# Norm weights spread by a product with ones, and a waiting expert's raw weights asked for behind unit 1's rows

## The chip, the cores and the metric

The kernel runs on one core of one Trainium2 chip. The core has five engines that run side by side and wait for each other through semaphores: TensorE (PE, matmul), VectorE (DVE), ScalarE (ACT), GpSimd (POOL) and SyncE (SP, which issues DMAs); sixteen DMA engines move the data. The metric is device time in microseconds of one execution. Times of runs are given as medians; durations of single instructions come from one profiled execution.

## What is computed

One layer of a hybrid trunk on x of 512 rows and 1024 columns, fp32 in and out. It is a norm, a combined projection into three mixers, an output product, then a mixture of experts, then a last norm:

```python
h = rms_norm(x, norm1_g[l])
proj = h @ w_in[l]
y_ssm  = ssm_mixer(proj[..., :s0], ...)        # 256 columns, diagonal state space, GLU
y_pool = pool_mixer(proj[..., s0:s1], ...)     # 256 columns, causal means over 2, 4, 8, 16
y_att  = moba_attention(q, k, v, rel_bias)     # 8 heads of 64, blocks of 256, relative bias
x = x + concatenate([y_ssm, y_pool, y_att]) @ w_out[l]
h = rms_norm(x, norm2_g[l])
x = x + hier_moe(h, ...)                       # 4 groups of 4 experts, best group, best 2 in it
return rms_norm(x, final_norm_g)

def rms_norm(x, g):
    y = xf * lax.rsqrt(jnp.mean(xf * xf, axis=-1, keepdims=True) + RMS_EPS)
    return y * g
```

Each expert is `silu(h @ w_gate) * (h @ w_up) * weight @ w_down` with 256 inner columns.

## The kernel before

Rows are worked on in four blocks of 128 (`NT`). Products with large weights are made in fp16: each fp32 weight half tile (128 x 1024, 512 KB) is loaded into one of five staging slots (`STG`) and split into a high and a low fp16 part, and a product runs in three passes (high·high, high·low, low·high). The high part is made by ScalarE; the low part by VectorE in one SCALAR_TENSOR_TENSOR or, where `less_busy(1.0)` finds VectorE over 1 us more loaded than GpSimd in the planner's model, by GpSimd, for which ScalarE makes one more pass that scales the slot in place.

The order of all work is set when the program is built. `Flow` (L71 on) is a planner: every stage is a coroutine that yields the engine it wants, the events it needs and the tokens (buffers) it takes; the planner keeps a modelled time for each engine and for DMA, and lets the coroutine go that can start first, by rank where several can. Changing one stage's needs or cost can so move any other instruction on any engine, and can change which splits go to GpSimd.

Start: `s_first_loads` (L419) issues on SP the four x blocks and the small constants; `s_norm1` (L495) takes the squares (ScalarE), the scale (GpSimd) and the product with the scale and the norm weights `g1` (VectorE, tile `xp`), then 8 transpositions (`pt`) and the split into `hT`. The weights of the projection follow as v, u, q, k, p, q, k, v (tiles `w_v`, `w_u`, `w_q`, `w_k`, `w_p`, products `ps_v`, `pu`, `ps_q`, `ps_k`, `ps_p`). Meanwhile VectorE prepares the SSM's powers (`sm`, `pw`, `bb`, `bl`) and the attention's bias: a one-hot product `pb` of two parts is copied from PSUM into `scr`, SP stores it (`t_scr`) and reads it back in eight broadcast DMAs (`tb`). `psS` are attention scores, `pr` probabilities, `ptp` their transpositions.

Experts: after the second norm and the routing, GpSimd scatters the rows into `x_scr` by expert (96 slots for each of 16 experts). They are worked on in units of 128 slots: unit 0 holds expert 0 and 32 slots of expert 1, unit 1 64 of expert 1 and 64 of expert 2, and so on. Unit 0 is gathered on chip by products (`gb`); later units read their rows from `x_scr` (`s_xt`, L1605, tile `xr`, for unit 1 in `xp_123`), transpose them (`tx`, then `xts`), make gate and up products (`pg`), Silu (`xs`), its transposition (`pta`, `aT`), the down product (`py`), and scatter `ys` to `y_scr`. The weights of experts come through the five slots in order (`s_exp_loads`), each with gate, up and down in two half tiles. Gate and up of experts 5 and 6 (`RAW`) are loaded without a split into spare pages (`s_raw_loads`, L1548, tile `raw`) while the attention's weights give their space free; they are split later into pages that earlier units have done with: expert 5 into that of expert 0, 6 into raw 5's, expert 7 into raw 6's. `s_xt` needs the scatters to have landed. All loads but GpSimd's scatters are issued by SP, in the order in which they stand.

## Time and profile before

| what | value |
|---|---|
| time, median of 3 runs | 431.93 us (429.52 to 432.06) |
| the profiled execution | 431.17 us, its span 429.4 us |
| TensorE busy | 364.4 us (85%) |
| VectorE busy | 321.7 us (75%) |
| ScalarE busy | 236.1 us (55%) |
| GpSimd busy | 54.6 us (13%) |
| moved by DMA | 110.33 MB, 257 GB/s in the mean |
| granted TensorE clock, mean | 0.949 |

The span is what the profiler records between first and last instruction; 1.8 us of the profiled execution lie around it. In a timeline each row is a start, a duration, an engine, a line (nearly all L96, a helper that records every operation), the operation with its output and inputs, and in brackets how long the engine sat idle before it and what released it. A row with x2 or more groups neighbours. SPq is SP's queue of issues: its durations are those of issuing, not of the transfer.

### The profile page before, as it was taken

The page shows a single profiled execution, that of the slowest core. Times are in us where ns is not written, and L with a number is a line of the kernel's source. Part 1 is how long each engine was busy: PE and PEld are TensorE (multiplying, and loading weights), DVE is VectorE, ACT ScalarE, POOL GpSimd, SP SyncE. Part 2 cuts the span into 40 slices and gives each one's busy share as a digit, 9 for nine tenths or more (in the row PEclk, how much of TensorE's full clock was granted, in tenths as well). Part 3 has the DMA queues.
Part 4 walks back from the last instruction along what each step waited for, and adds up shares of the span by engine and source line. Part 5 has one row for each costly group of instructions (what it writes and reads, how often), then busy time and mean ns, then how long its engine had stood idle before and what let it go on. Part 6 is the DMA issues. An engine that isn't in the chain of part 4 may idle for free.

```text
span 429.4 us, 8450 instructions
## 1 busy us (share of the span) xinstructions
PE 364.4 (85%) x3272; PEld 204.9 (48%) x3272; DVE 321.7 (75%) x649; ACT 236.1 (55%) x400; POOL 54.6 (13%) x87
## 2 busy tenths in 40 slices
PE   2799897399998999999799878699999875678991
PEld 1598453164454466554376754345445431333340
DVE  2798866967854778777578887989788887777382
ACT  4754132346757796937463216867677756565131
POOL 1200000420500000000034520122111010000020
PEclk9999999599999999999899988899999998689997
DMA  8935599950798998558855899838999997989924
GB/s 278 354 115 151 167 146 187 380 168 4 157 181 262 300 355 312 182 156 268 302 197 204 299 418 351 288 118 291 404 331 359 406 337 256 321 279 350 396 97 152
DMA packets 49384, 110.33 MB, mean 257 GB/s; under 512 B 4507, under 2 KB 25755, under 8 KB 49340
## 3 DMA queue, kind: packets, MB, share of 16 engines
q1 hardware_dynamic: 46188, 100.07, 72.1%
q0 software_dynamic: 2592, 9.44, 5.4%
q10 hardware_dynamic: 560, 0.25, 0.5%
q8 instruction: 27, 0.44, 0.4%
q14 instruction: 17, 0.14, 0.1%
HBM read 85.04 MB, written 24.69 MB: 256 GB/s over the span
## 4 chain that ended last, share of the span: by engine, by line
PE 50%; DMA 24%; DVE 13%; ACT 5%; issue 4%; SPq 1%; POOL 0%; POOLq 0%; ACTq 0%; DVEq 0%
PE px L96 7%; DMA st_lde<-in_moe_w_down_dram 7%; PE pg L96 6%; PE py L96 5%; DMA st_lde<-in_moe_w_gate_dram 4%; PE pf L96 4%; PE ps_v L96 4%; DVE gu L96 4%; DMA st_lde<-in_moe_w_up_dram 4%; DMA xs<-in_glu_w_dram 3%; PE psS L96 3%; PE pu L96 3%; PE ptp L96 3%; PE ps_k L96 3%; DVE dn L96 2%
## 5 line engine op out<-in xcount | busy, mean ns | idle before, releaser
L96 DVE SCALAR_TENSOR_TENSOR gu<-st_lde,gu 128x1024 f16<-128x1024 f32 x55 | 68.0, 1251 | 15.9 <-ACT gu L96 15.6
L96 PE MATMUL pg<-gu,xts 128*32 128x512 f16 (+1 forms) x960 | 71.7, 395 | 8.6 <-ACT gu L96 7.2
L96 ACT ACTIVATE gu<-st_lde 128x1024 f16<-128x1024 f32 x56 | 58.2, 1056 | 16.4 <-DMA st_lde<-in_moe_w_up_dram 11.1
L96 PEld LDWEIGHTS <-xts 128*32 128x32 f16 (+1 forms) x960 | 31.1, 103 | 44.0 <-issue 20.4
L96 PE MATMUL px<-wo,cat 128*128 128x512 f16 x192 | 45.6, 389 | 2.4 <-ACT wo L96 1.8
L96 PE MATMUL py<-dn,aT 128*32 128x512 f16 (+1 forms) x480 | 39.0, 420 | 8.8 <-ACT aT L96 7.5
L96 DVE SCALAR_TENSOR_TENSOR dn<-st_lde,dn 128x1024 f16<-128x1024 f32 x32 | 38.6, 1218 | 2.4 <-ACT dn L96 1.8
L96 ACT ACTIVATE dn<-st_lde 128x1024 f16<-128x1024 f32 x32 | 33.2, 1053 | 7.6 <-DMA st_lde<-in_moe_w_down_dram 7.5
L96 PEld LDWEIGHTS <-hT 128*64 128x64 f16 (+1 forms) x384 | 30.7, 155 | 5.1 <-issue 1.4
L96 PEld LDWEIGHTS <-cat 128*128 128x128 f16 x192 | 18.9, 100 | 24.3 <-issue 6.0
L96 PEld LDWEIGHTS <-aT 128*32 128x32 f16 (+1 forms) x480 | 14.8, 105 | 30.1 <-ACT aT L96 9.7
L96 ACT ACTIVATE pr<-pr,nm 128x128 f32<-128x128 f32 (+3 forms) x32 | 17.9, 562 | 15.0 <-DVE nm L96 14.8
L96 POOL DMA_INDIRECT y_scr<-ys,tok x10 | 11.9, 1190 | 103.9 <-ACT ys L96 78.6
L96 PE MATMUL ps_v<-w_v,hT 128*128 128x256 f16 x192 | 24.1, 282 | 1.0 <-ACT hT L96 0.6
L96 PE MATMUL ps_q<-hT,w_q 128*128 128x512 f16 x96 | 22.6, 380 | 0.0
L96 PE MATMUL ps_k<-hT,w_k 128*128 128x512 f16 x96 | 22.2, 380 | 0.0
L96 PE MATMUL ptp<-cpk,pr 128*128 128x128 f32 x80 | 13.6, 284 | 9.5 <-DVE pr L96 9.3
L96 DVE CUSTOM_DVE_ANT_0 pr<-psS,tb 128x128 f32<-128x128 f32 (+3 forms) x32 | 15.5, 485 | 7.7 <-DMA xs<-in_glu_w_dram 3.8
L96 ACT COPY pts<-ptp 128x128 f32<-128x128 f32 (+3 forms) x32 | 12.7, 424 | 12.5 <-PE ptp L96 12.4
L96 PEld LDWEIGHTS ptp<-cpk,pr 128*128 128x128 f32 x80 | 9.2, 141 | 17.4 <-DVE pr L96 9.4
L96 ACT ACTIVATE xs<-xp 128x512 f32<-128x512 f32 (+1 forms) x12 | 9.2, 770 | 14.5 <-DVE xp L96 10.7
L96 DVE TENSOR_TENSOR xts<-tx,xts 128x512 f16<-128x512 f32 x22 | 14.7, 685 | 2.4 <-ACT xts L96 2.1
(242 smaller groups left out, 633.3 us busy)
## 6 DMA issues: line engine op xcount, KB each, us to landing
st_lde<-in_moe_w_down_dram SPq DMA_DIRECT2D x32, 512.0 KB
st_lde<-in_moe_w_gate_dram SPq DMA_DIRECT2D x28, 512.0 KB
st_lde<-in_moe_w_up_dram SPq DMA_DIRECT2D x28, 512.0 KB
x_scr<-zero SPq DMA_DIRECT2D x12, 512.0 KB
xr<-x_scr SPq DMA_DIRECT2D x10, 512.0 KB
xp<-in_x_dram SPq DMA_DIRECT2D x8, 512.0 KB
y_scr<-zero SPq DMA_DIRECT2D x8, 512.0 KB
yr<-y_scr SPq DMA_DIRECT2D x4, 1024.0 KB
```

The lines of the kernel that those rows point to most:

```text
L96: r = f(*args, **kw)
```

## The change

The norm weights are no longer broadcast by a DMA of 128 x 1024. One row of 1 x 1024 is loaded first on SP, ahead of x; two fp32 products of a row of ones with its halves write it to all partitions in PSUM, and VectorE copies them into `g1`. The raw loads of expert 6 wait also for the event that unit 1's rows have been asked for.

```diff
     def s_first_loads():
+        yield "sp"
+        sp.dma_start(g1[0:1, :], a["norm1_g"])
+        fl.sig_dma("g1r")
         for t in range(NT):
...
             if t == 0:
-                yield "sp"
-                sp.dma_start(g1, a["norm1_g"].to_broadcast([P, D]))
-                fl.sig_dma("g1")
                 yield "sp"
                 sp.dma_start(cpk, a["cpk"])
...
+    def s_g1():
+        one = scr_a[0:1, 0:P]
+        yield "dve"
+        v.memset(one, 1.0)
+        for nh in range(2):
+            half = slice(nh * 512, (nh + 1) * 512)
+            yield "pe", ("g1r",), ("mm",)
+            pg = bank("mm", f"pg1_{nh}")
+            pe.matmul(pg, one, g1[0:1, half], start=True, stop=True)
+            yield "dve"
+            v.tensor_copy(g1[:, half], pg)
+            fl.give("mm")
+        fl.sig("g1")
...
-                    yield "sp", (("wo_end", 1),), ("fly",)
+                    yield "sp", (("wo_end", 1),) if e == RAW[0] else (("wo_end", 1), "xr_rows"), ("fly",)
...
             fl.sig_dma(("xr", u))
+            if u == NG:
+                fl.sig("xr_rows")
...
     fl.spawn(2, s_first_loads())
+    fl.spawn(0, s_g1())
```

The planner then orders the program anew. Seven splits go to GpSimd where one did: both halves of `w_q` and the first of `w_k` of the first pair of heads, one gate half of expert 2, one down half of expert 5, and two halves (gate and up) of expert 7, which had one there already.

VectorE, start, before: the first rows that read x or weights (`xp` is an x block times its scale and `g`, first block 0; `w_v` the low half of the first weights; `hT` the low half of x's transposition).

```order
L96 SCALAR_TENSOR_TENSOR xp_122<-xp_122,rs_174,g_126 128x1024
L96 SCALAR_TENSOR_TENSOR w_v_179<-st_ld_v_0_157,w_v_179 128x1024
L96 SCALAR_TENSOR_TENSOR hT_111<-pt_0_182,hT_110 128x4x128
L96 SCALAR_TENSOR_TENSOR hT_111<-pt_1_189,hT_110 128x4x128
L96 SCALAR_TENSOR_TENSOR w_v_179<-st_ld_v_1_159,w_v_179 128x1024
L96 SCALAR_TENSOR_TENSOR xp_122<-xp_122,rs_199,g_126 128x1024
```

And now:

```order
L96 MEMSET scr_112 1x128
L96 COPY g_126<-pg_0_169 128x512
L96 COPY g_126<-pg_1_175 128x512
L96 SCALAR_TENSOR_TENSOR w_v_183<-st_ld_v_0_158,w_v_183 128x1024
L96 SCALAR_TENSOR_TENSOR xp_122<-xp_122,rs_181,g_126 128x1024
L96 SCALAR_TENSOR_TENSOR w_v_183<-st_ld_v_1_160,w_v_183 128x1024
```

The first split of w_v has moved ahead of x block 0.

VectorE, the end of the bias preparation, before (`w_k` is a split, `ptu` a transposition of u, `pb` the two bias products; the store of the table waits for the second copy of `pb`):

```order
L96 COPY bbd<-bb 64x16x16 x2
L96 SCALAR_TENSOR_TENSOR w_k_648<-st_ld_k_0_416,w_k_648 128x1024
L96 TENSOR_TENSOR scr_112<-bb,pw 128x1024
L96 COPY xp_123<-ptu_651 128x512
L96 TENSOR_TENSOR bl_682<-bb,pw 128x1024
L96 SCALAR_TENSOR_TENSOR w_k_648<-st_ld_k_1_419,w_k_648 128x1024
L96 COPY xp_123<-ptu_684 128x512
L96 TENSOR_TENSOR bl_682<-bl_682,scr_112 128x1024
L96 COPY scr_113<-pb_645 128x512
L96 COPY scr_113<-pb_723 128x127
```

And now:

```order
L96 COPY bbd<-bb 64x16x16 x2
L96 COPY scr_113<-pb_613 128x512
L96 TENSOR_TENSOR scr_112<-bb,pw 128x1024
L96 TENSOR_TENSOR bl_691<-bb,pw 128x1024
L96 SCALAR_TENSOR_TENSOR w_k_668<-st_ld_k_1_427,w_k_668 128x1024
L96 COPY xp_123<-ptu_674 128x512
L96 TENSOR_TENSOR bl_691<-bl_691,scr_112 128x1024
L96 COPY scr_113<-pb_695 128x127
L96 COPY xp_123<-ptu_705 128x512
```

The first split of w_k is gone from VectorE (it is GpSimd's, as are both of w_q further up), the first copy of pb stands earlier, and one copy of ptu stands behind the second pb copy. On TensorE, in the same part of the program, the six `ps_p` products that stood ahead of the first `ptp` stand behind it.

SP at the first expert units, before (`raw_0` and `raw_1` are gate and up of experts 5, then 6; `st_lde_2` a down half; `flag` a word that SP reads; `xp_123<-x_scr` the rows of unit 1, `xr` those of units 2 and on):

```order
L96 DMA raw_1_2627<-in_moe_w_up_dram 128x1024 x2
L96 DMA raw_0_2648<-in_moe_w_gate_dram 128x1024 x2
L96 DMA raw_1_2704<-in_moe_w_up_dram 128x1024 x2
...
L1912 TENSOR_LOAD flag
...
L96 DMA st_lde_2_0_2912<-in_moe_w_down_dram 128x1024
L96 DMA st_lde_2_1_2915<-in_moe_w_down_dram 128x1024
L96 DMA xp_123<-x_scr 128x1024
L96 DMA xr_2945<-x_scr 128x1024
```

And now:

```order
L96 DMA raw_1_2638<-in_moe_w_up_dram 128x1024 x2
L96 DMA st_lde_2_0_2734<-in_moe_w_down_dram 128x1024
L96 DMA st_lde_2_1_2768<-in_moe_w_down_dram 128x1024
L1931 TENSOR_LOAD flag
...
L96 DMA xp_123<-x_scr 128x1024
L96 DMA raw_0_2906<-in_moe_w_gate_dram 128x1024 x2
L96 DMA raw_1_2915<-in_moe_w_up_dram 128x1024 x2
L96 DMA st_lde_2_0_2928<-in_moe_w_down_dram 128x1024
L96 DMA xr_2942<-x_scr 128x1024
```

The read of unit 1's rows has moved ahead of expert 6's raw loads and of its down halves. On TensorE the eight `tx` of unit 1 have moved from behind unit 0's `py` to directly behind `pm`, ahead of unit 0's `pta`.

VectorE in the same part, behind unit 1's `pg`, before: the four splits of raw 6 (`raw_0_2648`, `raw_1_2704`) stand ahead of unit 1's `ys`.

```order
L96 SCALAR_TENSOR_TENSOR gu_1_3091<-raw_0_2648,gu_0_3090 128x4x256 x2
L96 SCALAR_TENSOR_TENSOR xs_124<-pg_3049,xs_124 128x256
L96 TENSOR_TENSOR xts_2925<-tx_0_3119,xts_2925 128x512
L96 SCALAR_TENSOR_TENSOR gu_1_3091<-raw_1_2704,gu_0_3090 128x4x256
L96 SCALAR_TENSOR_TENSOR aT_3205<-pta_3167,aT_3205 128x256
L96 TENSOR_TENSOR xts_2925<-tx_1_3162,xts_2925 128x512
L96 SCALAR_TENSOR_TENSOR gu_1_3091<-raw_1_2704,gu_0_3090 128x4x256
L96 TENSOR_SCALAR ys_3210<-py_0_3211,cw 128x512
L96 SCALAR_TENSOR_TENSOR gu_1_3225<-st_lde_0_0_2947,gu_0_3224 128x4x256
```

And now:

```order
L96 SCALAR_TENSOR_TENSOR aT_3176<-pta_3132,aT_3176 128x256
L96 TENSOR_TENSOR xts_2938<-tx_1_3135,xts_2938 128x512
L96 TENSOR_SCALAR ys_3185<-py_0_3186,cw 128x512
L96 SCALAR_TENSOR_TENSOR gu_1_3129<-raw_0_2906,gu_0_3128 128x4x256 x2
L96 SCALAR_TENSOR_TENSOR gu_1_3129<-raw_1_2915,gu_0_3128 128x4x256 x2
L96 SCALAR_TENSOR_TENSOR xs_124<-pg_3141,xs_124 128x256
L96 TENSOR_TENSOR xts_125<-tx_0_3286,xts_125 128x512
L96 SCALAR_TENSOR_TENSOR gu_1_3327<-st_lde_0_0_3004,gu_0_3326 128x4x256
```

The four splits have moved behind `ys`; expert 7's first split (`st_lde_0_0`) follows them in both.

## Rows read from the trace of the kernel before

**Rows 1.** The page, part 2: busy tenths of TensorE and the rate of DMA in 40 equal slices of the span, 10.7 us each.

```profile
PE   2799897399998999999799878699999875678991
...
GB/s 278 354 115 151 167 146 187 380 168 4 157 181 262 300 355 312 182 156 268 302 197 204 299 418 351 288 118 291 404 331 359 406 337 256 321 279 350 396 97 152
```

**Rows 2.** The timeline of the first 15 us: SP's issues of x block 0 and of the norm weights, the square of x block 0 on ScalarE, its product with scale and norm weights on VectorE, the first weight split's two halves, and the square of x block 2.

```profile
0.73 0.39 SPq L96 DMA_DIRECT2D xp<-in_x_dram  x1
...
1.18 0.42 SPq L96 DMA_DIRECT2D g<-in_norm_g_dram  x1
...
4.22 1.06 ACT L96 ACTIVATE xs<-xp 128x1024 f16<-128x1024 f32 x1 [2.21 <-DMA xp<-in_x_dram]
...
6.37 1.28 DVE L96 SCALAR_TENSOR_TENSOR xp<-xp,rs,g 128x1024 f32<-128x1024 f32 x1 [5.48 <-POOL rs L96]
...
8.67 1.06 ACT L96 ACTIVATE w_v<-st_ld_v 128x1024 f16<-128x1024 f32 x1 [3.29 <-DMA st_ld_v<-in_w_in_dram]
...
9.76 1.23 DVE L96 SCALAR_TENSOR_TENSOR w_v<-st_ld_v,w_v 128x1024 f16<-128x1024 f32 x1 [2.11 <-ACT w_v L96]
...
14.31 1.06 ACT L96 ACTIVATE xs<-xp 128x1024 f16<-128x1024 f32 x1 [1.63 <-DMA xp<-in_x_dram]
```

**Rows 3.** The view that groups instructions by shape: the fp32 products and the PSUM copies that are nearest to those that the change adds (count, busy us, mean ns of one, idle before).

```profile
L96 PE MATMUL pf<-yr,cpk 128*128 128x512 f32 x16 | 7.7, 592 | 0.0
...
L96 DVE COPY xp<-ptu 128x512 f32<-128x512 f32 x2 | 1.4, 682 | 0.0
```

**Rows 4.** The timeline of 28 to 55 us: three splits on VectorE (w_q, w_k), the copy of the second bias product, SP's store of the bias table and the first two of its eight broadcasts.

```profile
29.98 1.22 DVE L96 SCALAR_TENSOR_TENSOR w_q<-st_ld_q,w_q 128x1024 f16<-128x1024 f32 x1
...
41.66 1.22 DVE L96 SCALAR_TENSOR_TENSOR w_k<-st_ld_k,w_k 128x1024 f16<-128x1024 f32 x1 [0.67 <-ACT w_k L96]
...
49.85 0.29 DVE L96 COPY scr<-pb 128x127 f32<-128x127 f32 x1 [0.63 <-PE pb L96]
...
50.17 0.35 SPq L96 DMA_DIRECT2D t_scr<-scr  x1
...
52.38 1.00 SPq L96 DMA_DIRECT2D tb<-t_scr  x2
```

**Rows 5.** The timelines of TensorE and VectorE at 70 to 82 us: the last products before TensorE's stall, the first probabilities on VectorE, the first transposition of them on TensorE.

```profile
71.30 1.46 PE L96 MATMUL ps_p<-hT,w_p 128*128 128x512 f16 x6
...
81.71 0.48 PE L96 MATMUL ptp<-cpk,pr 128*128 128x128 f32 x1 [8.95 <-DVE pr L96]
```

```profile
73.81 0.29 DVE L96 CUSTOM_DVE_ANT_0 pr<-psS,tb 128x128 f32<-128x128 f32 x1 [3.79 <-DMA xs<-in_glu_w_dram]
```

**Rows 6.** VectorE and GpSimd side by side, in their timelines: operations of 504 elements at 75 to 78 us, and splits at 284 to 291 us.

```profile
75.61 3.46 POOL L96 TENSOR_TENSOR xp<-xp,ph 128x504 f32<-128x504 f32 x2
...
287.00 2.14 POOL L96 TENSOR_TENSOR gu<-st_lde,gu 128x1024 f16<-128x1024 f32 x1 [17.27 <-ACT gu L96]
```

```profile
76.59 1.46 DVE L96 TENSOR_TENSOR xp<-xp,ph 128x504 f32<-128x504 f32 x1
...
284.91 1.21 DVE L96 SCALAR_TENSOR_TENSOR gu<-raw,gu 128x1024 f16<-128x1024 f32 x1
...
287.24 2.98 DVE L96 SCALAR_TENSOR_TENSOR gu<-st_lde,gu 128x1024 f16<-128x1024 f32 x1
```

**Rows 7.** SP's issues of the first and the last raw half tiles and of unit 1's rows, the last row scatter on GpSimd, the view of windows for 252 to 260 us (its length, then busy us of PE, PEld, DVE, ACT and POOL with instructions, granted clock, DMA share, GB/s), and the page's list of DMA issues for the last two scatters (median us to landing).

```profile
236.24 0.80 SPq L96 DMA_DIRECT2D raw<-in_moe_w_gate_dram  x2
...
240.43 1.18 SPq L96 DMA_DIRECT2D raw<-in_moe_w_up_dram  x2
...
261.77 0.33 SPq L96 DMA_DIRECT2D xp<-x_scr  x1
```

```profile
248.93 1.60 POOL L96 DMA_INDIRECT x_scr<-xs,slot_i  x1 [0.19 <-issue]
...
252.00:260.00 8.00, 6.60 (x108) 4.04 (x107) 7.00 (x23) 1.60 (x2) 0.00 (x0) 0.98 1.03 421
...
x_scr<-xs,slot_i POOLq DMA_INDIRECT x2, 12.1
```

**Rows 8.** TensorE's timeline at the first units: pm and py of unit 0, tx of unit 2, pg of unit 1.

```profile
258.82 1.98 PE L96 MATMUL pm<-vals,place 128*128 128x36 f32 x16
...
263.08 4.21 PE L96 MATMUL py<-dn,aT 128*32 128x512 f16 x48 [1.40 <-ACT aT L96]
...
271.83 1.33 PE L96 MATMUL tx<-cpk,xr 128*128 128x128 f32 x8 [3.51 <-DVE xts L96]
273.09 6.93 PE L96 MATMUL pg<-gu,xts 128*64 128x512 f16 x48
```

**Rows 9.** Unit 1's ys on VectorE (the last split of raw 6 stands in rows 6, at 284.91), and SP's issues of expert 7's last half and of expert 8's first two.

```profile
286.57 0.75 DVE L96 TENSOR_SCALAR ys<-py,cw 128x512 f32<-128x512 f32 x1 [0.45 <-PE py L96]
```

```profile
289.17 0.33 SPq L96 DMA_DIRECT2D st_lde<-in_moe_w_down_dram  x1
290.25 1.79 SPq L96 DMA_DIRECT2D st_lde<-in_moe_w_gate_dram  x2
```

**Rows 10.** The view of windows for three stretches of the expert units (columns as in rows 7).

```profile
276.00:292.00 16.00, 16.00 (x202) 7.61 (x198) 14.06 (x15) 11.76 (x16) 3.39 (x3) 0.99 0.44 143
296.00:308.00 12.00, 11.46 (x143) 5.44 (x134) 9.21 (x12) 7.35 (x11) 1.44 (x2) 1.00 1.03 415
308.00:328.00 20.00, 20.00 (x296) 9.65 (x296) 17.25 (x21) 14.69 (x21) 2.22 (x4) 1.00 0.96 333
```

## The prediction

> **What bounds the kernel now.** I read the page's slices first, then the timelines of the start, of 28 to 55 us, of the attention's begin and of the first expert units, and last the windows behind them. No single limit holds for the whole span. The slices show TensorE near full in most of them, with a gap in the eighth (75 to 86 us) and thin ones near the end, and a DMA rate that swings between 4 and 418 GB/s [rows 1]: the stages have different limits, and the change must be priced in three of them.
>
> *Start.* VectorE's first large step (norm of x block 0) runs at 6.37; its first weight split starts at 9.76, after ScalarE has waited 3.29 us for the weights' landing, and ScalarE waits again 1.63 us for x block 2 [rows 2]. From 9.76 on VectorE is nearly always busy, and the scale and bias work of the SSM and of the attention queues up behind it.
>
> *Bias table.* The second bias product is copied out at 49.85, SP stores the table at 50.17 and asks for its eight broadcasts at 52.38 [rows 4]. The first attention block that needs them reaches VectorE at 73.81, after 3.79 us of idleness; TensorE has nothing left after 72.76 and starts the first transposition of probabilities only at 81.71, after 8.95 us of idleness [rows 5]. The broadcasts run at a fixed pace behind that store, so what moves the store moves the end of this stall.
>
> *First expert units.* Eight raw half tiles of 512 KB (experts 5 and 6) are issued from 236.24 to 241.6, in front of the down weights and of the last two row scatters; the read of unit 1's rows is issued only at 261.77, when the last scatter has landed [rows 7]. DMA runs at 421 GB/s meanwhile: it is the limit there. TensorE then gets unit 1's gate and up products from 273.09 to 280.02 [rows 8]. After that TensorE is full, DMA nearly idle (143 GB/s in 276 to 292, staging slots not free), then full again from 296 at 415 GB/s, 333 in 308 to 328 [rows 10]. From 296 the stream of weights is what the units wait for.
>
> **The change, part by part.**
>
> *Norm weights.* The 512 KB broadcast goes; a 4 KB row, two fp32 matmuls and two PSUM copies come. By the nearest rows these cost 2 × 0.59 on TensorE and 2 × 0.68 on VectorE [rows 3], 2.5 us together. TensorE does nothing before its first product and VectorE idles 5.48 us before 6.37 [rows 2], so they lie in the cover of x block 0's landing: cost nothing; without that cover 2.5 us. The row goes first on SP, so x block 0 is asked for 0.45 us later (the distance of the first two issues). The gain: 0.52 MB less ahead of the first weights, 1.4 us at the rate of the second slice (354 GB/s), so w_v lands near 7.3 instead of 8.67 and x block 2 near 12.9. But the first w_v split now stands ahead of x block 0's norm on VectorE: that norm moves from 6.37 to about 9.6 (7.3, plus one ScalarE pass of 1.06, plus a split of 1.23). From its first split on, VectorE has the same queue as before plus that norm: it starts 1.4 earlier and carries 1.28 more. I take 0; bounds −1.4 (all of the landing is kept) and +1.3 (none).
>
> *Bias chain.* In the changed order four operations leave VectorE's queue ahead of the second bias copy: two w_q splits, one w_k split (1.22 each) and one PSUM copy (0.68); and the first bias copy stands earlier, so the 0.63 us of waiting for the second product goes [rows 3, 4]. That is 3.66 + 0.68 + 0.63 = 4.97 us. The three splits go to GpSimd instead. What that does to VectorE the trace shows once for a split: a GpSimd split took 2.14 from 287.00, and the VectorE split that started at 287.24 took 2.98, where its neighbour took 1.21: 1.77 lost. The same is seen with 504-element operations: 1.46 on VectorE beside GpSimd [rows 6]. Three times 1.77 is 5.3, so the store moves by +0.3. Bounds: not blocked at all, −4.97; blocked for each whole GpSimd operation, 3 × 2.14 − 4.97 = +1.45. I take +0.3, since VectorE has work queued throughout that stretch, as at 287. The Trainium skill (SBUF — State Buffer, section "SBUF: two separate sides") says that VectorE and GpSimd share one port pair as an exclusive lock, and that an operation of VectorE with two SBUF inputs waits for the whole GpSimd operation. The row agrees nearly (1.77 of the 1.90 us that were left); by the rule the term would be +1.45.
>
> To this comes an order effect: six ps_p matmuls (1.46 us at 71.30) that filled TensorE ahead of the stall stand behind the first ptp now [rows 5]. The slices from 86 to 204 show TensorE at 8 or 9 tenths and more [rows 1], so they cost their 1.46. Together +1.8 (bounds −3.5 and +2.9). The rest of the order between 80 and 240 is reshuffled with the same work; I take 0.
>
> *First units.* Without expert 6's raw loads 2.1 MB less stand ahead of the last scatters: 5.0 us at 421 GB/s, so unit 1's rows are asked for near 256.8 and have landed by 260.3 (x block 0 took 3.5 from issue to use [rows 2]). tx of unit 1 now stands right behind pm, which ends near 260.8, so it doesn't wait. Against this, VectorE has the last split of expert 4 ahead of unit 0's gating and the e5 down split ahead of aT (1.2 each), and GpSimd splits beside it: py of unit 0 starts near 265, not 263.08. Then TensorE has 4.2 (py) + 6.2 to 6.9 (pg) + 1.3 (tx) without the idle 3.51 and the late tx: unit 1 ends near 277, 3 us earlier than 280.02 (bounds 1.5 and 6).
>
> *What is late next.* The four splits of raw expert 6 stand behind unit 1's ys on VectorE now, where before all four stood ahead of it [rows 6, 9]. ys comes 6 us after pg (Silu, pta, tx, 32 pg and 12 py products): near 283; four splits end near 288; before, the last ended at 286.1. They hold the page of expert 7, whose splits free the slots for expert 8. Before, SP asked for e7's last half at 289.17 and for e8 at 290.25, the first of them on GpSimd's split [rows 9]; now these come between 288 and 292, so the stream restarts where it did. The lead of 3 us then meets a stream that is full from 296. It can give back only where DMA is not full: 308 to 328 ran at 333 GB/s instead of 415 [rows 10], worth 20 × (1 − 333/415) = 4.0 us at most. I take 3.0, the lead itself. Bounds: −5.5 and, with the restart 2.5 late and nothing regained, +2.5.
>
> Sum: 0 + 1.8 − 3.0 = −1.2. The profiled execution took 431.17 (span 429.4 and 1.8 around it); 430.0 in its terms. It lies 0.76 under the median of the runs, 431.93, so 430.7 there.
>
> **The rivals.**
>
> *Faster: both gains stay.* If GpSimd's splits find VectorE in operations that don't collide (small ones, PSUM reads), the store comes 4.97 earlier and the stall ends 3.5 earlier even after the ps_p; and if the lead of unit 1 pulls the whole stream, another 4 to 5.5. That gives 423 to 425. For it: much of VectorE's work in the stretch of the bias is on 8 to 128 elements, and DMA at 143 GB/s in 276 to 292 is room that anything earlier could fill. Against it: the row at 287.24.
>
> *The landing doesn't come earlier.* If x_scr's last two scatters are slow by themselves (12.1 us to landing is their median [rows 7]) and not because of the raw loads, the read of unit 1 stays at 261 and tx, now ahead of pta on TensorE, holds up unit 0: unit 1 ends where it did; 431 + 1.8 = 433.5, still within 1%. Against it: DMA at 421 GB/s there is full.
>
> *Slower: GpSimd's splits are the bound.* Seven splits go to GpSimd, before one. If each blocks VectorE for its whole 2.14, the stall's end moves by +2.9; and expert 8's second load waits for GpSimd's split of e7's last up half, which has two ScalarE passes of 1.06 and 2.14 in front: the restart slips by 3, and no lead is regained. 431.9 + 2.9 + 2.5 to 3 gives 437 to 438. It decides if SP's e8 loads come after about 294 in the old clock. For it: 287.24 again; against it: GpSimd had idled for 17.27 us before that one split, so it has room [rows 6].
>
> **How the numbers follow.** A measurement of this kernel can tell about 1% (4.3 us) from no change: the shown runs spread over 2.5. Chances: my forecast 0.40 and the slow landing 0.10, both within 1% but for a few hundredths at either edge; both gains kept, or most of them, 0.32; GpSimd as the bound 0.18. So faster by over 1% 0.33, within 1% 0.49, slower 0.18. The range leaves out the last half of each outer case: 424 to 436.5. The likeliest case alone holds 427.7 to 433.5.
>
> **What would show it.** Norm: VectorE's first norm near 9.6 to 11 and pu within 1 us of 28.3. Bias: t_scr's store within 1.5 us of 50.2, VectorE's operations of 584 elements stretched beside GpSimd's splits, first ptp at 82 to 84.5. Units: the read of unit 1's rows 4 to 6 us earlier against unit 0's pg, unit 1's pg ending 2 to 6 earlier by the same measure, but e8's first loads within 2.5 of where they were, and DMA in the 20 us behind 308 above 333 GB/s. It is wrong if the store comes near 46, if e8 is asked for before 287, or if TensorE's idleness between 82 and 240 grows by more than 2 us through the new order, for which I took nothing.

## The result, and the profile after

The changed kernel took 437.36 us, median of 20 runs (431.69 to 441.99), beside 431.77 for 20 runs of the kernel before on the same chips: ratio 1.0139, 95% interval 1.0105 to 1.0174. It is slower by more than 1%, and above the forecast range of 424 to 436.5. A ratio in this document is that of the executions of either kernel that were not markedly slower than its fastest, so it can lie up to 0.7 of a point above the quotient of the medians. The profiled execution of the changed kernel took 435.24 us, span 433.3; the rows below are from it.

The start, timeline of TensorE, VectorE and ScalarE (columns as in [rows 2]):

```profile
2.36 3.75 PE L96 MATMUL pg<-g,scr 1*128 1x512 f32 x4 [2.36 <-DMA g<-in_norm_g_dram]
6.14 0.69 DVE L96 COPY g<-pg 128x512 f32<-128x512 f32 x1 [1.01 <-PE pg L96]
8.31 1.06 ACT L96 ACTIVATE w_v<-st_ld_v 128x1024 f16<-128x1024 f32 x1 [2.72 <-DMA st_ld_v<-in_w_in_dram]
9.40 1.23 DVE L96 SCALAR_TENSOR_TENSOR w_v<-st_ld_v,w_v 128x1024 f16<-128x1024 f32 x1 [2.56 <-ACT w_v L96]
10.54 1.28 DVE L96 SCALAR_TENSOR_TENSOR xp<-xp,rs,g 128x1024 f32<-128x1024 f32 x1
```

The spreading is done at 6.83. The weights of v are used from 8.31, where [rows 2] had 8.67: 0.36 us earlier, not 1.4. The norm of x block 0 stands behind the first split, at 10.54. TensorE begins `pu` at 29.24, 0.98 later than before (28.26).

The stretch of the bias table, TensorE, GpSimd, VectorE and SP in order of time, and then the end of the stall on TensorE (answering to [rows 4, 5]):

```profile
29.24 9.87 PE L96 MATMUL pu<-w_u,hT 128*64 128x256 f16 x160
31.84 4.93 POOL L96 TENSOR_TENSOR w_q<-st_ld_q,w_q 128x1024 f16<-128x1024 f32 x2 [11.60 <-ACT w_q L96]
32.47 2.30 DVE L96 TENSOR_SCALAR s1b<-scr 128x584 f32<-128x584 f32 x1
34.80 2.59 DVE L96 SCALAR_TENSOR_TENSOR scr<-s1b,scr 128x584 f32<-128x584 f32 x1
47.04 2.33 POOL L96 TENSOR_TENSOR w_k<-st_ld_k,w_k 128x1024 f16<-128x1024 f32 x1 [10.27 <-ACT w_k L96]
47.95 2.51 DVE L96 SCALAR_TENSOR_TENSOR w_k<-st_ld_k,w_k 128x1024 f16<-128x1024 f32 x1 [0.56 <-ACT w_k L96]
52.42 0.35 SPq L96 DMA_DIRECT2D t_scr<-scr  x1
82.05 0.45 PE L96 MATMUL ptp<-cpk,pr 128*128 128x128 f32 x1 [6.25 <-DVE pr L96]
83.59 2.74 PE L96 MATMUL ps_p<-hT,w_p 128*128 128x512 f16 x6
```

Beside GpSimd's two splits of w_q, VectorE's operations of 584 elements take 2.30 and 2.59 where the same ones, a few us earlier in this trace, take 0.47 and 0.77; beside that of w_k a split takes 2.51, where it took 1.22 [rows 4]. The store of the table comes 2.25 later than before, but the stall ends only 0.34 later (82.05 for 81.71), and the six `ps_p` behind it run for 2.74 at a granted clock of 0.50 (the lower level, 1.2 GHz), where they took 1.46 ahead of it [rows 5].

The first expert units, SP's issues, then TensorE, then VectorE (answering to [rows 7 to 9]; the last two rows of `pg` are the last two of three pieces of unit 1, each of 1.92; the transpositions between them are those of a later unit):

```profile
260.38 0.33 SPq L96 DMA_DIRECT2D xp<-x_scr  x1
260.77 0.89 SPq L96 DMA_DIRECT2D raw<-in_moe_w_gate_dram  x2
294.01 4.27 SPq L96 DMA_DIRECT2D st_lde<-in_moe_w_gate_dram  x2
...
254.40 5.80 PE L96 MATMUL pg<-gu,xts 128*32 128x512 f16 x96
264.18 1.06 PE L96 MATMUL tx<-cpk,xp 128*128 128x128 f32 x8 [2.08 <-DMA xp<-x_scr]
272.20 1.92 PE L96 MATMUL pg<-gu,xts 128*64 128x512 f16 x16
274.05 0.66 PE L96 MATMUL tx<-cpk,xr 128*128 128x128 f32 x4
274.64 1.92 PE L96 MATMUL pg<-gu,xts 128*64 128x512 f16 x16
...
283.17 4.62 DVE L96 SCALAR_TENSOR_TENSOR gu<-raw,gu 128x1024 f16<-128x1024 f32 x4
```

Stages are best compared behind unit 0's first product (254.40 here, 253.53 before). By that clock the rows of unit 1 are asked for at +5.98, before at +8.24; unit 1's `pg` ends at +22.2 (276.56), before at +26.5 (280.02): 4.3 us earlier. The four splits of raw 6 stand behind it and end at 287.79; expert 8's first load is asked for at +39.6, before at +36.7.

Two windows of the kernel before by the same clock (the last of its products behind; columns as in [rows 10]):

```profile
253.50:261.50 8.00, 7.59 (x114) 4.94 (x113) 6.58 (x25) 1.67 (x2) 0.00 (x0) 1.00 1.04 410
313.50:333.50 20.00, 20.00 (x288) 9.77 (x280) 17.76 (x22) 15.45 (x22) 2.49 (x4) 1.00 0.98 353
393.50:408.50 15.00, 14.96 (x159) 6.35 (x160) 7.19 (x11) 4.12 (x7) 0.00 (x0) 1.00 1.01 400
```

and of the changed one, with rows of the timelines of ScalarE, VectorE and TensorE:

```profile
254.40:262.40 8.00, 7.70 (x113) 4.34 (x112) 7.52 (x24) 4.76 (x5) 0.94 (x1) 0.94 0.61 237
314.40:334.40 20.00, 15.66 (x220) 7.65 (x216) 15.60 (x19) 14.06 (x20) 2.60 (x4) 0.90 1.01 380
394.40:409.40 15.00, 14.96 (x171) 5.69 (x164) 6.02 (x9) 4.64 (x7) 0.00 (x0) 0.86 0.92 351
...
328.53 1.06 ACT L96 ACTIVATE gu<-st_lde 128x1024 f16<-128x1024 f32 x1 [2.85 <-DMA st_lde<-in_moe_w_gate_dram]
329.62 1.23 DVE L96 SCALAR_TENSOR_TENSOR gu<-st_lde,gu 128x1024 f16<-128x1024 f32 x1 [2.68 <-ACT gu L96]
330.76 0.42 DVE L96 SCALAR_TENSOR_TENSOR xs<-pg,xs 128x256 f32<-128x256 f32 x1
331.23 0.70 PE L96 MATMUL pta<-cpk,xs 128*128 128x128 f32 x2 [2.93 <-DVE xs L96]
392.64 0.70 PE L96 MATMUL pta<-cpk,xs 128*128 128x128 f32 x2 [4.24 <-DVE xs L96]
```

TensorE was full from +60 to +80 before; now it works 15.66 of 20 us there, at a clock of 0.90. The lead of 4.3 us at unit 1 is gone at unit 6, whose `pta` (331.23) ends at +77.5, before at +76.8. TensorE waits 2.93 there for `xs`, which on VectorE stands behind a weight split; that split waits 2.68 for its ScalarE half, and ScalarE waits 2.85 for the gate half tile to land. TensorE's last product ends at +170.7, before at +166.8. DMA stands at 237 GB/s in the first 8 us, where it ran at 410.

### The profile page after: what moved, and what is told of

The parts are those of the page before. It is cut to its first block, busy times and chain, and to the rows that moved or that the text cites. A ratio compares the mean times of both kernels' runs of the same rounds, so it can differ in the third digit from the quotient of the medians.

```text
span 433.3 us, 8476 instructions
## 1 busy us (share of the span) xinstructions
PE 370.4 (85%) x3276; PEld 205.9 (48%) x3276; DVE 323.5 (75%) x646; ACT 244.4 (56%) x407; POOL 73.1 (17%) x93
## 5 line engine op out<-in xcount | busy, mean ns | idle before, releaser
L96 DVE SCALAR_TENSOR_TENSOR gu<-st_lde,gu 128x1024 f16<-128x1024 f32 x53 | 65.5, 1251 | 12.9 <-ACT gu L96 12.6
L96 PE MATMUL pg<-gu,xts 128*32 128x512 f16 (+1 forms) x960 | 69.6, 391 | 2.6 <-ACT gu L96 2.5
L96 PEld LDWEIGHTS <-xts 128*32 128x32 f16 (+1 forms) x960 | 29.9, 101 | 38.1 <-issue 13.5
L96 PE MATMUL py<-dn,aT 128*32 128x512 f16 (+1 forms) x480 | 42.1, 447 | 5.2 <-ACT aT L96 4.8
L96 DVE SCALAR_TENSOR_TENSOR dn<-st_lde,dn 128x1024 f16<-128x1024 f32 x31 | 39.7, 1300 | 7.5 <-ACT dn L96 7.5
L96 PE MATMUL px<-wo,cat 128*128 128x512 f16 x192 | 44.0, 380 | 0.7 <-DVE wo L96 0.7
L96 POOL DMA_INDIRECT y_scr<-ys,tok x10 | 14.8, 1478 | 95.7 <-ACT ys L96 84.1
L96 PE MATMUL pta<-cpk,xs 128*128 128x128 f32 x24 | 6.4, 355 | 14.8 <-DVE xs L96 14.8
L96 POOL TENSOR_TENSOR gu<-st_lde,gu 128x1024 f16<-128x1024 f32 x3 | 6.6, 2213 | 72.1 <-ACT gu L96 72.1
```

The costliest lines, as they stand in the source:

```text
L96: r = f(*args, **kw)
```

## The experiments

Each kernel was timed in turn with the kernel before. There are three groups, with medians of before of 432.63, 432.13 and 433.37 us. Kernels are compared by their medians, those of different groups by the distance from before's median of their own group.

**The two edits apart.** `norm_only` is the changed kernel with

```diff
-yield "sp", (("wo_end", 1),) if e == RAW[0] else (("wo_end", 1), "xr_rows"), ("fly",)
+yield "sp", (("wo_end", 1),), ("fly",)
```

and `raw_only` the kernel before with that line the other way round; the planner orders each anew.

> The norm row alone, planned anew: it keeps the changed order up to the first expert unit (three splits of w_q and w_k on GpSimd) and the old order behind it. Theory G (GpSimd's splits block VectorE: in the bias preparation, and later at expert 7, where the restart of the weight stream also comes late): unit 0 starts 1 to 2.5 us later as in the changed kernel, and the end moves by as much: 432.5 to 434.5. Theory F (the front makes the whole loss, the experts only carry it): 436 to 437.

> The later raw loads alone, planned anew: the old order up to the first expert unit, the changed one behind it. Theory G: the lead of 3 us at unit 1 is lost when expert 8 is asked for 3 to 4 us late; the end comes 3 to 4 us later than before, 434.5 to 436. Theory F: the lead stays, 428 to 430.

Measured: `norm_only` 434.80, ratio 1.0104 (1.0061 to 1.0146), 0.3 above the range of Theory G; `raw_only` 434.51, ratio 1.0057 (1.0025 to 1.0090), at the lower edge of it. By the medians the halves lose 2.2 and 1.9 us of the whole's 5.6, by the ratios 1.04 and 0.57 of 1.39 points: there is a loss in each, and neither gains.

**The spreading by itself.** `norm_fixed` keeps the order of before row by row and only replaces the broadcast (the row, two products, two copies, ahead of x block 0's norm; a cut in a diff is marked by three dots).

```diff
-sp.dma_start(g1, a["norm1_g"].to_broadcast([P, D]))
...
+pe._real.matmul(pg, one, g1[0:1, nh * 512:(nh + 1) * 512], start=True, stop=True)
+v._real.tensor_copy(g1[:, nh * 512:(nh + 1) * 512], pg)
```

> The first norm's row and its spreading by two products, in the order of the kernel before: no work moves to GpSimd and no split changes its place. Theory O (the front's loss of 4.5 us is in the new order and in GpSimd's splits, the spreading itself is nearly free): within 1.5 us of before, 430.5 to 433; the first norm of x block 0 near 6.4 to 7, w_v's landing up to 1.4 us earlier. Theory E (the spreading itself costs, since its products run on a slow clock and the landing hardly comes earlier): 433.5 to 435.

Measured: 430.63 against 432.13, ratio 1.0026 (0.9981 to 1.0071): no loss that can be told, as Theory O has it. VectorE and ScalarE at the start of this kernel:

```profile
7.18 1.28 DVE L96 SCALAR_TENSOR_TENSOR xp<-xp,rs,g 128x1024 f32<-128x1024 f32 x1 [0.21 <-DVE g L434]
8.09 1.06 ACT L96 ACTIVATE w_v<-st_ld_v 128x1024 f16<-128x1024 f32 x1 [2.46 <-DMA st_ld_v<-in_w_in_dram]
```

The norm comes 0.81 later than in [rows 2], behind the second copy, and the weights are used 0.58 earlier. So what the first edit loses lies in the order and the splits that the planner made of it.

**GpSimd's splits.** In the order of the changed kernel, row by row, VectorE makes again all seven splits that went to GpSimd (`dve_all`), the three of w_q and w_k (`dve_win`), or the four of experts (`dve_exp`); ScalarE's extra pass for each goes too.

```diff
-act.activation(src, src, AF.Copy, scale=scale)
-act.activation(hi, src, AF.Copy)
...
-pool.tensor_tensor(lo, src, hi, ALU.subtract)
+act._real.activation(hi, src, AF.Copy, scale=scale)
...
+v._real.scalar_tensor_tensor(lo, src, scale, hi, ALU.mult, ALU.subtract)
```

> The changed order kept row by row, but all seven GpSimd splits made by VectorE in their places, and ScalarE's extra pass of each left out. Theory G: the bias table's store comes no later than in the changed kernel and the extra stretches on VectorE are gone, expert 8 is asked for 2 to 4 us earlier: 432 to 434. Theory O (the order is the loss, whichever engine splits): 436.5 to 438.5.

> The changed kernel, its order row by row; only the three splits of the window (two of w_q, one of w_k) that went to GpSimd are made by VectorE again, and ScalarE's extra pass for each is left out; GpSimd keeps its splits of expert weights. Theory W (VectorE held beside GpSimd in the front is most of what all seven splits cost): 433.5 to 435, about 3 us under the changed kernel. Theory X (the expert splits cost most): 436 to 437.5. In either case scr near 32.5 takes 0.8 and not 2.6.

> The changed kernel, its order row by row; only the four splits of expert weights that went to GpSimd are made by VectorE again, without ScalarE's extra pass; GpSimd keeps the three of the window. Theory W: 436 to 437.5, hardly under the changed kernel. Theory X (the expert splits hold up expert 8's loads and with them the stream): 433.5 to 435.

Measured: `dve_all` 433.72, ratio 1.0033 (0.9988 to 1.0078); `dve_win` 434.52, 1.0128 (1.0033 to 1.0223); `dve_exp` 440.13, 1.0243 (1.0142 to 1.0344). The first is in the range of Theory G, the second in that of W, the third in none. The three splits of the window carry what GpSimd's splits cost: with them on VectorE the time is 433.7 and 434.5, with them on GpSimd 437.4 and 440.1. The interval of `dve_win` alone doesn't part it from the changed kernel; that of `dve_all` does. The four of experts cost nothing that shows. That `dve_exp` came out above the changed kernel (six runs, 435.27 to 441.65) is not explained.

`norm_win` is `norm_only`, row by row, with the same three splits on VectorE.

> The first edit alone in its own order (as norm_only, row by row), with the three splits of the window that went to GpSimd made by VectorE. Theory W (those three splits are what the first edit loses): 428 to 431.5, under norm_only by 3 us or more and not above before. If the new order costs by itself: 433 to 435.

Measured: 430.06 against 433.37, ratio 0.9948 (0.9902 to 0.9995), 4.7 us under `norm_only`'s median (5.5 by the distances from before). It is the fastest kernel of the study: well under `norm_only`, and under before by a margin that the interval just clears. VectorE, TensorE (`pu`'s second part) and SP in it:

```profile
32.62 0.46 DVE L96 TENSOR_SCALAR s1b<-scr 128x584 f32<-128x584 f32 x1
33.12 0.77 DVE L96 SCALAR_TENSOR_TENSOR scr<-s1b,scr 128x584 f32<-128x584 f32 x1
39.23 2.19 PE L96 MATMUL pu<-w_u,hT 128*64 128x256 f16 x32
45.31 1.22 DVE L96 SCALAR_TENSOR_TENSOR w_k<-st_ld_k,w_k 128x1024 f16<-128x1024 f32 x1
48.49 0.35 SPq L96 DMA_DIRECT2D t_scr<-scr  x1
```

and the same places in `norm_only`, with the bias product ahead of `pu`'s second part and with ScalarE's copy of `pu` and its extra pass for w_k:

```profile
31.80 2.30 DVE L96 TENSOR_SCALAR s1b<-scr 128x584 f32<-128x584 f32 x1
34.13 2.60 DVE L96 SCALAR_TENSOR_TENSOR scr<-s1b,scr 128x584 f32<-128x584 f32 x1
38.39 0.49 DVE L96 TENSOR_TENSOR pw<-mag,ph 128x72 f32<-128x72 f32 x2 [0.85 <-ACT ph L96]
40.44 1.13 PE L96 MATMUL pb<-scr 33*128 33x512 f32 x2 [2.00 <-issue]
41.49 3.56 PE L96 MATMUL pu<-w_u,hT 128*64 128x256 f16 x32
45.10 0.60 ACT L96 ACTIVATE xp<-pu 128x512 f32<-128x512 f32 x1 [6.26 <-PE pu L96]
45.59 1.05 ACT L96 ACTIVATE st_ld_k<-st_ld_k 128x1024 f32<-128x1024 f32 x1
48.71 2.31 DVE L96 SCALAR_TENSOR_TENSOR w_k<-st_ld_k,w_k 128x1024 f16<-128x1024 f32 x1 [1.96 <-ACT w_k L96]
52.97 0.35 SPq L96 DMA_DIRECT2D t_scr<-scr  x1
```

The store is 4.48 later, 0.19 of it from an earlier place (`pu` starts at 28.57 against 28.38). Of the other 4.29, 4.76 are VectorE's three stretched operations (1.84 + 1.83 + 1.09), 2.81 its idleness behind ScalarE (0.85 + 1.96, which `norm_win` does not have: its rows there follow without a gap), less 3.66 for the three splits that left its queue: 3.91, the rest in small gaps.

The two idle stretches have different sources. The 0.85 is a wait for ScalarE's `ph` that `norm_win` has too, but there a split of w_q (34.61 to 35.83) covers it: moving that split away saved less than its 1.22. The 1.96 goes by way of TensorE. Its bias product `pb` starts 0.11 behind VectorE's copy of its input, which ends at 40.33 (37.73 in `norm_win`), after TensorE has stood idle for 2.00; behind that pause the rest of `pu` takes 3.56 at a granted clock of 0.54, nearly all of it at the lower level of 1.2 GHz, where it takes 2.19 at full clock in `norm_win`. So ScalarE's copy of `pu` starts 3.64 later, and the passes for w_k, with the extra one of 1.05 (45.59), stand behind it. In the changed kernel the same pause of 1.98 left the clock at 1.00 and `pu` at 2.19; VectorE's wait there is 0.56.

**Expert 6's loads in the old order.** `raw_fixed` keeps the order of before and issues the four raw loads of expert 6 behind the read of unit 1's rows; `raw_xr2` puts them behind that of unit 2's rows (`NG + 1` in the condition).

```diff
-stage_load(("lde", e, i, j), [source(e, i, j)], [4, FE], raw[:, j])
+late.append((stv, source(e, i, j)))
...
 sp.dma_start(xr, x_scr[u * P:(u + 1) * P, :])
+if u == NG:
+    for dst, src in late:
+        sp._real.dma_start(dst, src)
```

> The old order kept row by row on every engine, only expert 6's four raw loads stand on SP behind the read of unit 1's rows; the norm weights as before. If the late read by itself was the cost: unit 1's rows land 4 to 5 us earlier and the time falls by 2 to 4 us, 428 to 430. If TensorE's order holds unit 1 back (tx behind unit 0's py) and the stream is the limit behind it: within 1 us of before, 431 to 432.5.

> The order of the kernel before; only expert 6's four raw loads are moved on SP, behind the read of unit 2's rows, which itself follows that of unit 1's rows. Theory Q (what spoiled the earlier form of this was unit 2's rows queued behind 2.1 MB): no wait of 6.6 us for these rows on TensorE any more; unit 1's rows 1 to 5 us earlier, unit 1 ends 2 to 5 us earlier by unit 0's first product; the time 429 to 432. If the lead is lost again to the stream of weights, 431.5 to 433 with the same early units. Theory R (raw loads of expert 6 come too late for their own splits wherever they stand behind): ScalarE waits for them by 2 us or more near 275 and the time is 434 or more.

Measured: `raw_fixed` 438.69, ratio 1.0206 (1.0160 to 1.0253); `raw_xr2` 435.96, 1.0121 (1.0025 to 1.0217). The first missed both theories. SP and TensorE in it:

```profile
263.35 0.91 SPq L1609 DMA_DIRECT2D raw<-in_moe_w_gate_dram  x2
266.71 0.34 SPq L96 DMA_DIRECT2D xr<-x_scr  x1
277.74 1.94 PE L96 MATMUL tx<-cpk,xr 128*128 128x128 f32 x8 [6.60 <-DMA xr<-x_scr]
```

The rows of unit 2, asked for behind 2.1 MB, arrive 11 us later, and in the old order their transposition stands ahead of unit 1's products on TensorE, which waits 6.60 us. In `raw_xr2` that wait is gone and unit 1 ends 2.5 us earlier by unit 0's clock, as Theory Q has it, but a wait of 3.78 us, which Q did not expect, stands at the next rows behind:

```profile
283.91 0.63 PE L96 MATMUL tx<-cpk,xr 128*128 128x128 f32 x4 [3.78 <-DMA xr<-x_scr]
```

The time is over Q's ranges. Theory R has the time, but not by its cause: ScalarE waits for no raw tile by 2 us.

**Fewer bytes.** `raw_half` moves only expert 6's two up loads; `raw_skip` is `raw_only`, row by row, with 4 KB in each of the four loads, so expert 6 computes with a constant in place of its weights. The first pair of lines is that of `raw_half`, the second that of `raw_skip`, for expert 6.

```diff
-yield "sp", (("wo_end", 1),) if e == RAW[0] else (("wo_end", 1), "xr_rows"), ("fly",)
+yield "sp", (("wo_end", 1),) if e == RAW[0] or i == 0 else (("wo_end", 1), "xr_rows"), ("fly",)
...
-stage_load(("lde", e, i, j), [source(e, i, j)], [4, FE], raw[:, j])
+sp._real.dma_start(stv[0:1], source(e, i, j)[0:1])
+staged["lde", e, i, j] = cpk[:, None, 0:1].to_broadcast([P, 4, FE])
```

> The second edit alone, in its own order (as raw_only, row by row), but expert 6's four raw loads move 4 KB each instead of 512 KB; the splits of expert 6's gate and up weights read a constant instead, so expert 6 computes with other numbers. 2.1 MB less pass through the DMA engines. Theory D (what the second edit loses is DMA time: behind unit 0's first product the engines run at some 220 instead of 410 GB/s for 8 us, and the 2.1 MB are then carried in a stretch that is full): expert 8's loads come earlier, TensorE is full 60 to 80 us behind unit 0's first product (15.4 of 20 us busy in raw_only), and the time falls by 3 us or more under raw_only, to 428 to 431.5. Theory S (the late place of the splits on VectorE and the order behind them cost it, not the bytes): 433.5 to 435, as raw_only.

> The second edit for half of the bytes: expert 6's two gate loads are asked for as in the kernel before, only the two up loads behind the read of unit 1's rows. Theory D: DMA behind unit 0's first product runs at 300 GB/s or more in the 8 us instead of 220, about half of the lead of unit 1 stays, and the time lies between before and raw_only or under both, 430 to 433. Theory S: nearer raw_only or above, 434 to 436, as the order of the splits behind is again another.

Measured: `raw_skip` 434.35, ratio 1.0075 (1.0031 to 1.0118); `raw_half` 434.16, 1.0027 (0.9984 to 1.0071). `raw_half` does not decide: its ratio lies between before's and that of `raw_only`, as Theory D has it, its time in the range of Theory S. By `raw_skip` Theory D falls: without the 2.1 MB the time is that of `raw_only` (434.51), expert 8 is asked for at 292.32, +38.0 behind unit 0's first product (254.36) where `raw_only` has +37.6, and the gap of TensorE stays:

```profile
314.40:334.40 20.00, 16.57 (x240) 8.46 (x238) 16.90 (x22) 15.54 (x22) 2.72 (x5) 1.00 1.01 387
...
292.32 4.26 SPq L96 DMA_DIRECT2D st_lde<-in_moe_w_gate_dram  x2
```

What SP waits for before it issues loads, in the changed kernel, 292 to 390 us (total, times, longest):

```profile
SPq L96 <- DVE gu L96: 35.8, 24, 3.5
SPq L96 <- DVE dn L96: 18.4, 13, 4.8
```

and before, 290 to 386:

```profile
SPq L96 <- DVE gu L96: 33.4, 23, 3.9
SPq L96 <- DVE dn L96: 22.8, 14, 5.1
```

In both, SP spends 54 to 56 of some 97 us waiting for VectorE's splits to give staging slots back: a load is asked for when a slot comes free. That names only the last link of a slot's round. Worked out from the timelines, the last 49 half tiles of weights in the changed kernel take 9.9 us in the mean from issue to the end of the low split, and 6.7 of them pass before ScalarE takes the tile up; before, 10.1 and 6.9. Whether DMA or the splits set that round was not tested.

**Both edits, mended.** `win_half` is the changed kernel with the edits of `raw_half` and `dve_win`.

> Both edits, the second for half of the bytes as in raw_half, and the window's three splits on VectorE. Theories D and W together: 428 to 432, 5 us or more under the changed kernel. If the halves interfere: 433 to 436.

Measured: 431.57 against 433.37, ratio 1.0013 (0.9976 to 1.0051): no longer slower than before, and not under `norm_win`. It lies in the range of Theories D and W together although `raw_skip` speaks against D; why it is under `dve_win`, by 4.2 us in distance from before, was not taken apart.

The traces side by side, in us, without that of `raw_half`, whose profiled execution (437.44) was its longest. The columns are the start of `pu`; the store of the bias table behind it; unit 0's first product; then, all behind that product, expert 8's first load, the last load of weights, and the end of TensorE's last product; and the granted clock, mean from that last load to that end.

| kernel | w_q, w_k splits | expert 6's loads | pu | store | unit 0 | expert 8 | last load | end | clock |
|---|---|---|---|---|---|---|---|---|---|
| before | VectorE | ahead | 28.26 | 21.91 | 253.5 | 36.7 | 131.8 | 166.8 | 1.00 |
| norm_fixed | VectorE | ahead | 27.93 | 21.91 | 254.0 | 38.3 | 133.1 | 168.1 | 1.00 |
| raw_only | VectorE | moved | 28.41 | 21.91 | 256.0 | 37.6 | 132.8 | 169.2 | 0.95 |
| raw_fixed | VectorE | moved | 28.42 | 21.91 | 256.5 | 40.3 | 134.2 | 169.2 | 1.00 |
| raw_xr2 | VectorE | moved | 28.30 | 21.91 | 256.1 | 38.0 | 134.8 | 169.5 | 1.00 |
| raw_skip | VectorE | moved, 4 KB | 28.23 | 21.91 | 254.4 | 38.0 | 132.4 | 169.0 | 0.95 |
| norm_only | GpSimd | ahead | 28.57 | 24.40 | 257.5 | 36.8 | 130.7 | 165.4 | 1.00 |
| after | GpSimd | moved | 29.24 | 23.18 | 254.4 | 39.6 | 132.8 | 170.7 | 0.91 |
| dve_exp | GpSimd | moved | 28.80 | 24.42 | 256.5 | 38.1 | 134.3 | 170.7 | 0.95 |
| dve_all | VectorE, new order | moved | 29.63 | 20.10 | 251.6 | 38.0 | 133.8 | 170.2 | 0.95 |
| dve_win | VectorE, new order | moved | 29.23 | 20.11 | 252.6 | 41.0 | 137.5 | 171.5 | 1.00 |
| norm_win | VectorE, new order | ahead | 28.38 | 20.11 | 251.2 | 37.9 | 131.8 | 166.6 | 1.00 |
| win_half | VectorE, new order | half moved | 29.35 | 20.11 | 252.5 | 40.3 | 134.3 | 170.3 | 0.95 |

The two losses stand apart. Unit 0 starts at 252.0 in the mean of the four kernels with the new order and VectorE's splits, at 256.1 in the three with GpSimd's: 4.1 us. From there to the end it takes 166.7 in the mean of the four kernels that load expert 6 ahead, 170.0 in that of the nine others: 3.3 us, with no overlap between the sets.

The 3.3 come in three parts, in the means of the same two sets: expert 8 is first asked for at +37.4 and at +39.0 (1.6), the last weights at +131.8 and at +134.1 (0.7 more), and the end lies 34.9 and 35.9 behind that load (1.0). The last part goes with the clock: in the seven traces with a clock of 1.00 in the last column, 34.0 to 35.1 us pass from the last load to the end, in the six with 0.91 or 0.95, 36.1 to 37.9.

## Why the prediction was wrong

**Norm weights: about right.** I took 0. In the order of before the spreading costs nothing that can be told. In the new order `pu` starts 0.1 to 1.4 us later (28.26 before; `norm_win` 28.38, `dve_all` 29.63), at most a little over my upper bound of 1.3. The landing came 0.36 to 1.2 us earlier (8.31, in `norm_win` 7.45, for 8.67), not 1.4, and the two products took 3.75, three times the 1.18 that I had; that lies in the cover of x's landing but for some 0.6 us: in `norm_fixed` the scale is ready at 6.55 and the norm starts at 7.18, behind the second copy.

**Bias chain: right in its sum by luck, with a store that was 2 us out.** The store moved by +2.25, not +0.3. Of this 0.98 is the start; behind `pu` it moved by +1.27, and by up to +2.51 in the other kernels with these splits on GpSimd. The stretching was not larger than I had it (5.3 for three splits; 4.76 in `norm_only`; here 1.83 + 1.82 + 1.29 = 4.94). What I left out is VectorE's idleness behind ScalarE: 0.84 + 0.56 here, 0.85 + 1.96 in `norm_only`. With it my own sum comes out: 4.94 − 4.97 + 1.40 = +1.37 here, 4.76 − 4.97 + 2.81 = +2.60 there, for +1.27 and +2.49 measured. Part of it is that a split that I counted as saved had covered a wait; the other part runs over TensorE, whose `pb` waits for VectorE's late copy. And a saving was there without GpSimd: the new order with VectorE's own splits stores at 20.10, 1.81 earlier than before. Moving three splits of 1.22 off VectorE made the store 3.1 to 4.3 later, not 3.66 earlier.

The Trainium skill's rule (SBUF — State Buffer, section "SBUF: two separate sides") of an exclusive lock is what the rows of the changed kernel show: the operation that starts at 32.47, under the first of two splits, ends at 34.77, and the next, under the second, at 37.39, just behind that split's end at 36.77. The first of the two has only one tensor from SBUF as input, so the wait is not confined to operations with two, as I had put it. By that rule I had +1.45 for the store beside my +0.3. That +1.27 was measured behind `pu` is no proof of it: the +1.45 took 6.42 for the three stretches, which came to 4.94, and left out the idleness.

What moves the store does not move the end of the stall by as much, as I had assumed: in the other kernels of the new order the two moved together to within 1.5 us, here the stall ended 0.34 later for a store 2.25 later. The row from which I read that wait names another load than the broadcasts as what ended it [rows 5]. The six `ps_p` cost more than their 1.46, since behind the stall they ran at the lower clock (2.74). TensorE's idleness between 82 and 240, for which I took nothing, grew by 0.4. The front as a whole, which I put at +1.8, is +1.0 by the table (unit 0 at 256.1 in the mean, at 255.1 in the six kernels with the old order, which spread over 3.0) and +2.2 by the medians of `norm_only`.

**First units: right in size, not in the terms.** Unit 1's rows were asked for 2.3 us earlier by unit 0's clock, not 5.0, and TensorE waited 2.08 for them. Unit 1 ended 4.3 earlier all the same (forecast 3, bounds 1.5 and 6): the idle 3.51 ahead of `tx` [rows 8] is gone, and its `pg` took 3 × 1.92 = 5.76 us instead of 6.93.

**What is late next: the step that failed.** That expert 8's loads would not come earlier was right; they came 2.9 late, a little past the bound for it (2.5), which held in `dve_all` (1.3). What failed is the term of −3.0: that the stream of weights takes up the lead of unit 1, because DMA ran at 333 GB/s from 308 on and had room to 415. The row that I took this from has the DMA engines busy for a share of 0.96 there, beside 1.03 at 415 GB/s [rows 10], so it hardly shows room. What the runs show in its place: a load is asked for when a staging slot comes free, and a slot's round takes 9.9 us, as before (10.1). The loads did not come earlier but later, and unit 6 lost the lead in a wait that goes back to the landing of a gate half tile. DMA carried more in that stretch (380 GB/s, 353 before) without giving any of it back, and taking 2.1 MB out of the DMA engines left the loads and the time where they were. So the term was not −3.0 but +3.3 by the table: 1.6 from the late restart, 0.7 along the stream, 1.0 behind the last load. My upper bound for it, +2.5, was the loss of one late restart; that the end could come later than this I had not counted with.

With +1.0 in front and +3.3 behind, the traces hold 4.3 of the 5.6 us by which the medians rose; the rest is within what single executions differ by.

**The rivals.** "GpSimd's splits are the bound" gave 437 to 438 and came nearest to the time, with the right mechanism at the front. Behind, its mechanism was there but cost little: the restart came 2.9 late, with GpSimd's splits of expert 7 ending at 293.99 and 297.93, just ahead of the first two loads of expert 8 at 294.01 and 297.95 (293.1 and 297.1 in the old clock, on either side of the 294 from which I let it decide). With those splits on VectorE (`dve_all`) the restart is 1.6 earlier and the end 0.5 earlier; `dve_exp` gained nothing. Of "the landing doesn't come earlier" about half is true, since the read of unit 1's rows came 2.3 us earlier and not 5.0; its sum, 431 + 1.8, is 432.8 and not 433.5. Of "both gains stay" the lead of unit 1 came, but it did not pull the stream, and the store gained nothing.

**What stays open.** Why the restart is later and the stream loses 0.7 more on the way was followed in the rows, not tested; nor was what sets a slot's round. In the last 15 us of units the granted clock is 0.86 instead of 1.00, after TensorE had worked 5.76 of the 10 us ahead of them (7.92 before), with waits of 2.93 and 4.24 us in other places (rows above). That the clock makes the last 1.0 us goes with all thirteen traces, but no run changes the clock alone. In `raw_fixed` and `raw_xr2`, where the clock is full, the waits for the next rows stand ahead of the late stream.

## What to carry to other kernels

Before moving work off a busy VectorE to GpSimd, look at what VectorE would do beside it: here the three moved splits took more of VectorE's time away (4.94 us) than they freed (3.66), and their absence and lateness left VectorE waiting on top. Before a lead of one unit is booked as time, look at when the stream behind it asks for its loads, and on what: if it waits for buffers to come back, a DMA rate below the highest is no room that the lead can use. And when a planner reorders everything, time the edit once with the old order held fixed: here that told a harmless edit from a harmful order.

## What was not expected of the hardware

The two fp32 products of a single row took 3.75 us at 2.36, in four pieces, when TensorE had done nothing yet: 0.94 each, against 0.59 for pieces of fp32 products late in the kernel [rows 3], of which I had counted two. The granted clock of that stretch reads 1.00, so these rows do not say why.

After pauses of nearly the same length, 1.98, 2.00 and 1.97 us, the same 32 products of `pu` took 2.19 in the changed kernel at a granted clock of 1.00, but 3.56 in `norm_only` and 3.64 in `dve_exp` at 0.54 and 0.53. About as much, 1.2 us, lies between the stores of the table in these kernels.

With the same instructions in the same order up to unit 0, single executions reached it between 253.5 and 256.5 us. The granted clock behind the attention's stall (80 to 90 us) was 0.74 in the profiled execution of before, 0.65 in that of `raw_only` and 0.59 in that of `raw_fixed`. Before's profiled execution was the earliest of the six with that order at unit 0, which is why stages are compared by a clock of their own here.

A read of 512 KB that was queued behind 2.1 MB on SP arrived 11 us after its issue (266.71 to 277.74), where x block 0 took 3.5 [rows 2].
